# Channel mixers of a two-layer trunk: five plain hidden tiles in place of seven, and the down-projection's units placed by a list

## The chip, the cores and the metric

The kernel runs on one core of a Trainium2 chip. Its engines are TensorE (PE; its weight loads are listed apart as PEld), VectorE (DVE), ScalarE (ACT), GpSimd (POOL) and SyncE (SP), and in this kernel SP issues the weight loads. Every engine takes its own instructions in order; semaphores order the engines against each other. The metric is the device time of one execution in microseconds; a shorter time is better. Matmuls write into banks of PSUM, and ACT and DVE read from there.

## The reference, cut to what matters

The trunk has two layers. Each has a mixer over the sequence (a matrix memory in the first, banded attention in the second, both with attention to a memory) and then a channel mixer, on 512 tokens of width 1024 in float32. Only the channel mixers are touched by the change:

```python
D_FF = ((8 * D_MODEL // 3 + 127) // 128) * 128      # 2816, 22 tiles of 128
def conv_ffn(h, w_up, conv_w, conv_b, w_down):
    u, g = jnp.split(h @ w_up, 2, axis=-1)
    g = causal_dwconv(g, conv_w, conv_b)
    return (jax.nn.silu(g) * u) @ w_down
...
x = x + conv_ffn(rmsnorm(x, norm_ffn_g[l]), ffn_w_up[l], ffn_conv_w[l], ffn_conv_b[l], ffn_w_down[l])
```

So every hidden tile needs a gate product and an up product over all 1024 inputs, a causal convolution of width 3 along the sequence on the gate, a silu, and a multiplication. The 22 hidden tiles together then go through the down-projection.

## The kernel before

**Arithmetic.** A float32 product is made of three matmuls (`mm3`, L165 to L169): high by high, high by low, low by high. For that every weight tile and every activation is split in two: ACT casts the high half (L133), DVE subtracts it for the low half (L134). Weights arrive as raw float32 in a buffer of the pool `wr` (`load`), and `parts` splits them into a buffer of `wh` and one of `wl`; each of the three pools has three buffers. SP issues the loads in the order of the program, and a load waits until the split that last read its buffer is done. PSUM banks come from three pools, `mm` (three), `sc` (three) and `tr` (two), shown in the profile as `pmm`, `psc` and `ptr`.

**A channel mixer** (`ChannelMixer`, run once per layer, in the trace from about 285 to 605 us and from about 852 to 1170 us) takes the 22 hidden tiles in two ways.

*Plain tiles* (`plain`, the first seven): gate and up are each 8 × 3 matmuls of 128 × 512, 48 in a tile. The first four tiles use the unscaled input and multiply by the norm's row afterwards, on DVE (`L678`, `L684`); the later ones use the scaled forms in `ready`. The generator `forms` makes these: for each of the eight input tiles one multiply on DVE (`L693`) and a split, and then for four pairs the sums that Winograd's scheme wants (`L711`, halves of 256 columns) and their splits. `weave` mixes it into the plain tiles at a given rate. In this stage a scheduler orders the instructions.

*Winograd steps* (`step`, tiles 7 to 21): gate and up of a tile, seen as a 2 × 2 block product, take seven products instead of eight. A product is 4 × 3 matmuls of 128 × 256, 84 in a step. The weight sums and their splits for the next step are made meanwhile on DVE and ACT (`Forms`), and so is the convolution of the previous tile (`Tail`). In this stage the order of the code is the order of the instructions on PE, ACT and DVE (`manual_schedule`). The products go into three banks, `r1`, `r2` and `r3`. The middle of a step, with the lines of the profile:

```python
self.products(new.r3, w.s1, self.t(1), True)                       # L807
w.add_down(0)
then(tail, "split")
then(nxt, "split_up")
self.products(r1, w.s3, self.t(3))                                 # L811
A.copy(new.u3[:, :H], r1[:, :H])                                   # L812
V.tensor_tensor(out=new.pre[:, H:], in0=new.u3[:, :H], in1=new.r3[:, :H], op=ALU.add)   # L813
then(nxt, "split_sums")
w.down_products(1)
then(nxt, "sum_fourth")
w.add_down(1)
self.products(r1, w.a22, self.t(4))                                # L818
A.copy(new.pre[:, :H], r1[:, :H])                                  # L819
then(nxt, "split_down", "split_gate")
self.products(new.r3, w.s4, self.b(1, 1))
```

The product `a22` adds onto the same bank `r1` that the copy at L812 reads.

**The down-projection** of the first 16 hidden tiles is cut into 16 units. Unit q takes four hidden tiles (`GROUP`) and two output tiles: a load of 512 KB, a split, and two halves of 12 matmuls of 128 × 512 (`down_products`, in a `tr` bank). ACT copies each half out (`L735`), and POOL adds it to the output's spill with an accumulating transfer (`L736`). Units 0 and 1 stand behind plain tiles 5 and 6, units 2 to 15 in steps 7 to 20, one half after the product `s2` and one between `s3` and `a22`; step 21 has none. A unit's weights are loaded and split a step ahead. The last six hidden tiles go through their own final projection behind the mixer, whose matmuls the scheduler also puts into step 21.

`beside` issues, once per step, the transfers on POOL that build the bias rows of the later attention; only the first mixer has any.

Of the kernel before, what the change touches and what calls it, by code (L numbers as in the profile page):

```python
# [19 lines left out]
KT = D // P  # L20
# [18 lines left out]

PLAIN, UNSCALED, GROUP, LAST = 7, 4, 4, 6
H = S // 2


# [5 lines left out]
def trunk(  # L51
# [61 lines left out]
    for i, sel in enumerate(sels):  # L113
        G.memset(f(sel), 0.0)
        for s in (2 * i, 2 * i + 1):
            q = slice(32 * s, 32 * s + AH)
# [34 lines left out]
    def parts(raw, pinned=False):  # L151
        _, a, b = raw.shape
        hi = sb("wh", [P, D], F32R)[:, : a * b].rearrange("p (a b) -> p a b", a=a)
        lo = sb("wl", [P, D], F32R)[:, : a * b].rearrange("p (a b) -> p a b", a=a)
        split(hi, lo, raw, pinned=pinned)
        return hi, lo
# [25 lines left out]
    def run(gen):  # L182
        while True:
            try:
                next(gen)
            except StopIteration as end:
                return end.value

    def chain(*gens):
        for g in gens:  # L190
            yield from g
# [6 lines left out]
    def weave(job, filler, each, lead=0):  # L198

        due = lead  # L200
        for n in chain([0], job):
            due += each if n is None else each * n
            while due >= 1:
                due -= 1
                next(filler, None)

    def until(there, filler):
        while not there():
            next(filler)
# [35 lines left out]
    class Norm:  # L245


        def __init__(self):
            self.acc = self.row = None
# [154 lines left out]
    def reload_x():  # L404
        for j in range(KT):
            xT[j] = sb("u", [P, S])
            tc.keep_in_program_order(nc.sync.dma_start(xT[j], xspill[j]))
# [416 lines left out]
    class Forms:  # L824


        def __init__(self, mixer, j):
            self.mixer, n = mixer, KT // 2
            self.q = j - GROUP - 1
            self.up, self.gate = mixer.load_pair(j)  # L830
            self.raw_down = mixer.load_down(self.q) if self.q < 4 * n else None
            self.s13 = mixer.s[:, :D].rearrange("p (a b) -> p a b", a=KT)
            self.s24 = mixer.s[:, D : 2 * D].rearrange("p (a b) -> p a b", a=KT)

# [80 lines left out]
    def channel_mixer(l, act, norm, gain, beside):  # L915

        mixer = ChannelMixer(l, act, norm, gain, beside)
        forms = mixer.forms()
        run(mixer.plain(0))
        for j in range(1, UNSCALED):  # L920
            weave(mixer.plain(j), forms, KT / (16.0 * (UNSCALED - 1)))
        until(lambda: len(mixer.ready) == KT, forms) if len(mixer.ready) < KT else None
        mixer.buffers()
        for j in range(UNSCALED, PLAIN):
            q = j - GROUP - 1
            raw = mixer.load_down(q) if q >= 0 else None
            weave(mixer.plain(j), forms, 4 / (16.0 * 2))
            if raw is not None:
                w = parts(raw)
                for i in range(2):  # L930
                    mixer.add(*mixer.down_products(q, i, w))
        run(forms)
        mixer.later()
        reload_x()
        return mixer.hid[FT - LAST :]
# [289 lines left out]
    def more_rows():  # L1225
        if len(reps) < BH:
            bias_rows()

    hid = channel_mixer(0, act, norm, col["gffn"][:, 0:8], more_rows)
    norm2, kvact, act = Norm(), [], []  # L1230
    for j in range(KT):
# [161 lines left out]
    def final_norm(T):  # L1393
# [11 lines left out]
        nc.sync.dma_start(out[T * P : (T + 1) * P, S:], xt[T][1])  # L1405

    hid = channel_mixer(1, act, norm, col["gffn"][:, 8:16], lambda: None)
    n = LAST // 2
    for hf in range(2):
# [76 lines left out]
```

## Time and profile before

| | |
|---|---|
| median of 3 runs | 1211.17 us (1210.78 to 1211.25) |
| profiled execution | 1212.1 us, its span 1210.3 us |
| granted clock of TensorE, mean | 0.999 |
| PE busy | 1197.6 us, 99% of the span |
| PEld busy | 1054.6 us, 87% |
| DVE busy | 934.3 us, 77% |
| ACT busy | 693.0 us, 57% |
| POOL busy | 115.7 us, 10% |

The median is taken over runs without the profiler; the profile is of one further execution. The span is the time from the first to the last instruction of the trace. Engines' busy times overlap, so they don't add up to the span. A row of the timeline reads: start in us from the span's beginning, duration in us, engine, line, operation, tile written <- tiles read, shape; in brackets the idle time of the engine just before, and what released it. Matmuls are pipelined: a row's duration is longer than the distance to the next matmul's start, and that distance is the price of one. In a table of stretches (`A:B`) stand the length, then each engine's busy time with the number of its instructions, PE's granted clock, the share of the DMA engines and the GB/s.

### The profile page before, as it was taken

The page shows a single profiled execution, that of the slowest core. Times are in us where ns is not written, and L with a number is a line of the kernel's source. Part 1 is how long each engine was busy: PE and PEld are TensorE (multiplying, and loading weights), DVE is VectorE, ACT ScalarE, POOL GpSimd, SP SyncE. Part 2 cuts the span into 40 slices and gives each one's busy share as a digit, 9 for nine tenths or more (in the row PEclk, how much of TensorE's full clock was granted, in tenths as well). Part 3 has the DMA queues.
Part 4 walks back from the last instruction along what each step waited for, and adds up shares of the span by engine and source line. Part 5 has one row for each costly group of instructions (what it writes and reads, how often), then busy time and mean ns, then how long its engine had stood idle before and what let it go on. Part 6 is the DMA issues. An engine that isn't in the chain of part 4 may idle for free.

```text
span 1210.3 us, 18434 instructions
## 1 busy us (share of the span) xinstructions
PE 1197.6 (99%) x6919; PEld 1054.6 (87%) x6919; DVE 934.3 (77%) x1703; ACT 693.0 (57%) x1217; POOL 115.7 (10%) x191
## 2 busy tenths in 40 slices
PE   9999999999999999999999999999999999999997
PEld 8888888888889999999988888888888999999986
DVE  7878678878976777777788888997886677777755
ACT  4536567644545555555575767776464555555545
POOL 1300000000001111111011100001000101111100
PEclk9999999999999999999999999999999999999999
DMA  8634221444346667666563323236424666665551
GB/s 276 200 105 106 69 53 56 140 129 147 98 111 150 150 158 155 158 155 145 135 201 111 93 82 87 64 125 201 127 76 122 133 137 139 140 138 135 121 156 70
DMA packets 199019, 155.98 MB, mean 129 GB/s; under 512 B 7864, under 2 KB 179346, under 8 KB 198930
## 3 DMA queue, kind: packets, MB, share of 16 engines
q1 hardware_dynamic: 184338, 120.78, 34.0%
q0 software_dynamic: 14592, 34.03, 14.4%
q8 instruction: 54, 0.88, 0.3%
q14 instruction: 35, 0.29, 0.1%
HBM read 126.27 MB, written 32.44 MB: 131 GB/s over the span
## 4 chain that ended last, share of the span: by engine, by line
PE 92%; ACT 3%; DVE 3%; issue 0%; DMA 0%; SPq 0%; DVEq 0%; ACTq 0%
PE pmm L167 17%; PE pmm L169 17%; PE pmm L168 17%; PE ptr L167 6%; PE ptr L168 6%; PE ptr L169 6%; PE psc L167 6%; PE psc L169 6%; PE psc L168 6%; PE psc L505 2%; PE ptr L1313 1%; PE ptr L1334 1%; PE ptr L1335 1%; ACT wh L133 1%; DMA u<-in_mem_dram 0%
## 5 line engine op out<-in xcount | busy, mean ns | idle before, releaser
L167 PE MATMUL pmm<-u,wh 128*128 128x512 f32 (+1 forms) x952 | 336.0, 353 | 0.1
L169 PE MATMUL pmm<-u,wl 128*128 128x512 f32 (+1 forms) x952 | 332.5, 350 | 0.0
L168 PE MATMUL pmm<-u,wh 128*128 128x512 f32 (+1 forms) x952 | 332.2, 349 | 0.1
L134 DVE TENSOR_TENSOR wl<-wr,wh 128x1024 fp32r<-128x1024 f32 (+4 forms) x178 | 206.9, 1163 | 119.6 <-ACT wh L133 118.8
L133 ACT CAST wh<-wr 128x1024 fp32r<-128x1024 f32 (+4 forms) x178 | 178.4, 1004 | 131.6 <-PE pmm L168 50.3
L169 PEld LDWEIGHTS pmm<-u,wl 128*128 128x128 f32 x952 | 180.4, 189 | 22.3
L168 PEld LDWEIGHTS pmm<-u,wh 128*128 128x128 f32 x952 | 180.7, 190 | 19.3 <-DVE u L134 0.8
L167 PEld LDWEIGHTS pmm<-u,wh 128*128 128x128 f32 x952 | 180.5, 190 | 18.9 <-ACT u L133 0.5
L167 PE MATMUL ptr<-u,wh 128*128 128x512 f32 x272 | 106.7, 392 | 0.0
L168 PE MATMUL ptr<-u,wh 128*128 128x512 f32 x272 | 106.5, 392 | 0.0
L169 PE MATMUL ptr<-u,wl 128*128 128x512 f32 x272 | 105.8, 389 | 0.0
L736 POOL DMA_DIRECT2D xspill<-t x64 | 55.6, 868 | 472.6 <-ACT t L735 462.2
L167 PE MATMUL psc<-u,wh 128*128 128x512 f32 (+1 forms) x248 | 84.0, 339 | 0.0
L169 PE MATMUL psc<-u,wl 128*128 128x512 f32 (+1 forms) x248 | 83.8, 338 | 0.0
L168 PE MATMUL psc<-u,wh 128*128 128x512 f32 (+1 forms) x248 | 83.8, 338 | 0.0
L169 PE MATMUL pmm<-u,u 128*128 128x256 f32 x264 | 74.9, 284 | 0.2 <-DVE u L134 0.2
L167 PE MATMUL pmm<-u,u 128*128 128x256 f32 x264 | 75.0, 284 | 0.0
L168 PE MATMUL pmm<-u,u 128*128 128x256 f32 x264 | 74.8, 283 | 0.0
L735 ACT COPY t<-ptr 128x512 f32<-128x512 f32 x64 | 37.5, 586 | 63.2 <-PE ptr L169 63.2
L134 DVE TENSOR_TENSOR u<-t,u 128x512 fp32r<-128x512 f32 x78 | 53.4, 689 | 19.0 <-ACT u L133 18.7
L134 DVE TENSOR_TENSOR u<-pt,u 128x512 fp32r<-128x512 f32 x90 | 61.7, 689 | 5.1 <-ACT u L133 3.0
L133 ACT CAST u<-pt 128x512 fp32r<-128x512 f32 x90 | 55.4, 618 | 9.9 <-DVE pt L845 9.8
(285 smaller groups left out, 2431.2 us busy)
## 6 DMA issues: line engine op xcount, KB each, us to landing
wr<-in_ffn_w_up_dram SPq DMA_DIRECT2D x58, 512.0 KB, 4.6
wr<-in_ffn_w_down_dram SPq DMA_DIRECT2D x38, 512.0 KB, 3.7
xspill<-t POOLq DMA_DIRECT2D x64, 256.0 KB, 4.6
pt<-in_ffn_w_up_dram SPq DMA_DIRECT2D x30, 512.0 KB, 6.6
wr<-in_a_w_in_dram SPq DMA_DIRECT2D x20, 512.0 KB, 3.9
xspill<-u POOLq DMA_DIRECT2D x32, 256.0 KB, 3.0
u<-xspill SPq DMA_DIRECT2D x32, 256.0 KB, 5.1
wr<-in_w_kv_dram SPq DMA_DIRECT2D x12, 512.0 KB, 4.0
```

The source lines that it names most:

```text
L133: high = A.copy(hi, src) if on_act else V.tensor_copy(hi, src)
L134: low = V.tensor_tensor(out=lo, in0=src, in1=f(hi), op=ALU.subtract)
L167: nc.tensor.matmul(o, lh, rh, start=first, stop=False, skip_group_check=more)
L168: nc.tensor.matmul(o, lh, rl, start=False, stop=False, skip_group_check=more)
L169: nc.tensor.matmul(o, ll, rh, start=False, stop=last, skip_group_check=more)
L505: nc.tensor.matmul(o, a, b, start=first and i == 0, stop=i == 1)
L735: A.copy(t, o)
L736: G.dma_start(xspill[j], t, accum_op=ALU.add)
L1313: nc.tensor.transpose(tp[:, b * P : (b + 1) * P], es[T, h][:, b * P : (b + 1) * P], ident)
L1334: nc.tensor.matmul(o2[:, s * P :], w, hi_at(pts[h], s, s, TT - s), start=s == 0, stop=False)
L1335: nc.tensor.matmul(o2[:, s * P :], w, lo_at(pts[h], s, s, TT - s), start=False, stop=s == TT - 1)
```

## The change

Five plain tiles in place of seven, of which three instead of four are unscaled; tiles 5 and 6 become Winograd steps, so there are 17 steps instead of 15. A list `DOWN` says where each of the 16 units stands: units 0 and 1 both behind plain tile 4, unit 2 in step 6, unit 3 in step 8, units 4 to 15 in steps 9 to 20. Steps 5, 7 and 21 have none. The weights of units 0 and 1 are both loaded ahead of tile 4's. The eight scaled forms are woven into tiles 1 and 2 instead of 1 to 3, and the sums into tiles 3 and 4 instead of 4 and 5, at the same rate as before. `until` is called without its condition; it then draws from `forms` only while forms are missing, as before. Lines of the changed kernel are one to three higher than those of the kernel before.

```diff
-PLAIN, UNSCALED, GROUP, LAST = 7, 4, 4, 6
+PLAIN, UNSCALED, GROUP, LAST = 5, 3, 4, 6
+DOWN = (4, 4, 6, 8, *range(9, 21))
 H = S // 2
...
             self.mixer, n = mixer, KT // 2
-            self.q = j - GROUP - 1
             self.up, self.gate = mixer.load_pair(j)
-            self.raw_down = mixer.load_down(self.q) if self.q < 4 * n else None
+            self.raw_down = None
+            if j in DOWN:
+                self.q = DOWN.index(j)
+                self.raw_down = mixer.load_down(self.q)
...
         for j in range(1, UNSCALED):
             weave(mixer.plain(j), forms, KT / (16.0 * (UNSCALED - 1)))
-        until(lambda: len(mixer.ready) == KT, forms) if len(mixer.ready) < KT else None
+        until(lambda: len(mixer.ready) == KT, forms)
         mixer.buffers()
         for j in range(UNSCALED, PLAIN):
-            q = j - GROUP - 1
-            raw = mixer.load_down(q) if q >= 0 else None
-            weave(mixer.plain(j), forms, 4 / (16.0 * 2))
-            if raw is not None:
+            raws = {q: mixer.load_down(q) for q in range(len(DOWN)) if DOWN[q] == j}
+            weave(mixer.plain(j), forms, 4 / (16.0 * (PLAIN - UNSCALED)))
+            for q, raw in raws.items():
                 w = parts(raw)
                 for i in range(2):
                     mixer.add(*mixer.down_products(q, i, w))
```

## The prediction

> **What bounds the kernel now.** I read the page first, then the table of stretches and the list of waits for the two channel mixers, then the timeline around the first steps.
>
> ```profile
> span 1210.3 us, 18434 instructions
> PE 1197.6 (99%) x6919; PEld 1054.6 (87%) x6919; DVE 934.3 (77%) x1703; ACT 693.0 (57%) x1217; POOL 115.7 (10%) x191
> PEclk9999999999999999999999999999999999999999
> PE 92%; ACT 3%; DVE 3%; issue 0%; DMA 0%; SPq 0%; DVEq 0%; ACTq 0%
> ```
>
> TensorE (PE) is busy 99% of the span at a granted clock of nine tenths or more in every slice, and the chain that ended last is 92% PE. So an edit saves what it takes out of PE's own stream and costs what it makes PE wait. The two stages that it touches show this more sharply. In the table of stretches, one regular step with a down-projection unit and a stretch of the plain tiles read:
>
> ```profile
> core 0: us, PE busy (x) PEld busy (x) DVE busy (x) ACT busy (x) POOL busy (x), PEclk, DMA share, GB/s
> 294.40:319.80 25.40, 25.40 (x114) 21.01 (x113) 24.41 (x35) 14.94 (x21) 0.00 (x0) 1.00 0.33 99
> 371.67:387.22 15.55, 15.55 (x110) 14.56 (x108) 7.71 (x10) 7.55 (x13) 4.37 (x6) 1.00 0.68 156
> 387.22:402.77 15.55, 15.55 (x110) 14.57 (x109) 11.74 (x17) 8.80 (x17) 2.93 (x4) 1.00 0.67 156
> ```
>
> PE has no gap in any of them. DVE, 7.71 to 11.74 us of 15.55 in a step, has 24.41 of 25.40 us in the early plain tiles: there it is nearly as full as PE. The list of PE's waits has no entry between 285 and 605 us, nor between 852 and 1170 us. Nothing stalls before; the question is what stalls after.
>
> **1. Two plain tiles fewer, two Winograd steps more, in each mixer.** The timeline gives all prices of PE (first matmuls of plain tiles 3 and 4, of steps 7 and 8, and the edges of the two down halves of step 7):
>
> ```profile
> 317.26 0.39 PE L167 MATMUL pmm<-u,wh 128*128 128x512 f32 x1
> 328.14 0.39 PE L167 MATMUL pmm<-u,wh 128*128 128x512 f32 x1
> 371.67 0.28 PE L167 MATMUL pmm<-u,wh 128*128 128x256 f32 x1
> 375.98 0.40 PE L167 MATMUL ptr<-u,wh 128*128 128x512 f32 x1
> 378.73 0.28 PE L167 MATMUL psc<-u,wh 128*128 128x256 f32 x1
> 381.48 0.28 PE L169 MATMUL pmm<-u,wl 128*128 128x256 f32 x1
> 381.60 0.40 PE L167 MATMUL ptr<-u,wh 128*128 128x512 f32 x1
> 384.35 0.28 PE L167 MATMUL pmm<-u,u 128*128 128x256 f32 x1
> 387.22 0.28 PE L167 MATMUL pmm<-u,wh 128*128 128x256 f32 x1
> ```
>
> A plain tile takes 328.14 − 317.26 = 10.88 us, 48 matmuls of 512 columns. A step with its unit takes 387.22 − 371.67 = 15.55, its two down halves 378.73 − 375.98 and 384.35 − 381.60, 2.75 each; so its own 84 matmuls of 256 columns take 15.55 − 5.50 = 10.05. Each converted tile saves 10.88 − 10.05 = 0.83 us, four of them (two per mixer, two mixers) **3.3 us**. Number and price of the down units stay as they are, as do the final projections.
>
> The saving rests on 0.1196 us for a 256-column matmul (10.05 / 84) beside 0.2267 for 512 columns (10.88 / 48). The Trainium skill, "TensorE: Matmul & The Clock Gate", section "Wait — 56ns, not 53.3ns?", gives start-to-start as N over 2.4 GHz plus about 2.5 ns on a warm array. By that page, as an estimate, the pair would be 109 and 216 ns, a tile would save 1.2 us and the four 4.7. Both sizes are dearer here, the small one by more, so the measurement decides.
>
> **2. Steps without a down unit: a new wait on PE.** Only three units move. Before, q = 0 and 1 stand behind plain tiles 5 and 6 and q = 2 in step 7; after, 0 and 1 stand behind tile 4 and q = 2 in step 6. From step 8 on every step has the unit it had. Steps 5 and 7 have none, and this takes away what stands between product s3 (L811) and product a22 (L818). Both write the bank r1, and ACT's copy at L812 must read it between them. In step 7 of before:
>
> ```profile
> 381.80 0.37 ACT L812 COPY t<-pmm 128x256 f32<-128x256 f32 x1 [1.34 <-PE pmm L169]
> 382.20 0.42 DVE L813 TENSOR_TENSOR t<-t,psc 128x256 f32<-128x256 f32 x1 [0.49 <-ACT t L812]
> ```
>
> The last matmul of s3 starts at 381.48, the copy starts at 381.80, and what it releases can start at 382.20. The down half from 381.60 to 384.35 covers all of this. With no half there, a22 would want to start at 381.60 and be let go at 382.20: 0.60 us idle. Step 21, the one step of before that has no unit, shows the wait itself:
>
> ```profile
> 596.58 0.28 PE L169 MATMUL pmm<-u,wl 128*128 128x256 f32 x1
> 596.70 0.40 PE L167 MATMUL pmm<-u,wh 128*128 128x512 f32 x1
> 596.78 0.83 ACT L133 CAST wh<-wr 128x768 fp32r<-128x768 f32 x1 [0.93 <-PE pmm L168]
> 597.52 0.37 ACT L812 COPY t<-pmm 128x256 f32<-128x256 f32 x1
> 597.93 0.19 PEld L167 LDWEIGHTS pmm<-u,u 128*128 128x128 f32 x1 [0.35 <-ACT t L812]
> 597.93 0.39 PE L167 MATMUL pmm<-u,u 128*128 128x256 f32 x1
> 598.16 0.28 PE L168 MATMUL pmm<-u,u 128*128 128x256 f32 x1
> ```
>
> There a22's weight load is released by L812 at 597.93; PE meanwhile ran matmuls of the final projection, which steps 5 and 7 do not have at hand. It also shows the restart: 0.23 from the first to the second matmul, 0.11 above the usual 0.12. So a bare step costs 0.60 + 0.11 = 0.71 us, and four cost **2.8 us**. Bounds: nothing, if a22 need not wait (rival 1), and 597.93 − 596.70 = 1.23 each, 4.9 in all, if a cast stands ahead of the copy on ACT as it does in step 21. I take 0.71, because the casts of a regular step stand elsewhere: ACT was idle for 1.34 us when L812 began. The other waits on r1 keep a product of about 1.4 us between them.
>
> DVE in a bare step: step 5 is a first step, without the previous tile's taps, so it has the 7.71 us of the third row of the table beside 10.05 of PE. Step 7 has up to 11.74, more than PE's 10.05. DVE enters with slack, because step 6 leaves it 15.55. But its add at L813, which s4 waits for, then comes about 0.1 late: **0.2 us** for both mixers, with 0 and 11.74 − 10.05 − 0.71 = 1.0 each as ends.
>
> **3. Two raw down loads ahead of tile 4.** This is the tightest place. `load` has three raw buffers. Units 0 and 1 are now loaded before tile 4's weights and hold two of them until their splits, which stand behind tile 4's on DVE. So gate 4 and up 4 go one after the other through the third: load, cast, low half, next load. Before, two buffers took turns. The rows that price it:
>
> ```profile
> 294.35 0.69 DVE L678 TENSOR_TENSOR t<-pmm,rb 128x512 f32<-128x512 f32 x1
> 303.19 1.22 DVE L134 TENSOR_TENSOR wl<-wr,wh 128x1024 fp32r<-128x1024 f32 x1
> 304.32 0.68 DVE L134 TENSOR_TENSOR u<-t,u 128x512 fp32r<-128x512 f32 x1
> 304.92 0.74 DVE L645 SCALAR_TENSOR_TENSOR t<-t,cols,t 128x511 f32<-128x511 f32 x1
> 305.58 0.68 DVE L134 TENSOR_TENSOR u<-u,u 128x512 fp32r<-128x512 f32 x1
> 317.24 1.06 ACT L133 CAST wh<-wr 128x1024 fp32r<-128x1024 f32 x1
> 318.55 1.21 DVE L134 TENSOR_TENSOR wl<-wr,wh 128x1024 fp32r<-128x1024 f32 x1
> 319.79 0.37 SPq L146 DMA_DIRECT2D wr<-in_ffn_w_up_dram  x1
> 323.51 0.42 DVE L711 TENSOR_TENSOR t<-u 128x256 f32<-128x256 f32 x1
> 323.85 0.42 DVE L711 TENSOR_TENSOR t<-u,u 128x256 f32<-128x256 f32 x1
> DMA to landing us min/median/max: 3.4/3.8/4.9
> ```
>
> The first ten are timeline rows; the last is what the `wr` tiles between 308 and 353 us answer. Back to back, DVE takes 1.13 for a low half of 1024, 0.60 for a 512 subtract, 0.66 for a 512 multiply-add, 0.34 for a 256 subtract. The input's scaled forms now finish within tiles 1 and 2 instead of 1 to 3, so more stands ahead of up 3's low half. From 294.35 on I count 14 multiply-adds, 3 low halves of 1024, 19 subtracts or multiplies of 512 and 4 of 256 in the changed order: 9.24 + 3.39 + 11.40 + 1.36 = 25.39, so that low half starts at 319.74 (318.55 before) and ends at 320.95. The next load leaves 0.03 later (318.55 + 1.21 to 319.79). One round is 3.8 for landing, 1.06 cast, 1.21 low half and some 0.12 of hand-overs: 6.19. Gate 4 is ready at 327.14, before tile 4 wants it at 328.14, and up 4 at 333.33. PE wants up 4's low half with the third matmul of its 25th to 48th, at 328.14 + 5.44 + 0.45 = 334.03, and loads those weights one matmul earlier, at 333.80. That leaves 0.47 us, the same in both mixers. The count of DVE carries an error of a few tenths, so I take **0.1 us** per mixer, 0.2 in all; ends 0 and, with the slowest landing of the row twice, 2 × (4.9 − 3.8) − 0.47 = 1.7 per mixer.
>
> The Trainium skill, "DMA: Bandwidth & Descriptors", section "Anatomy of one DMA", states a fixed cost of about 2 us beside the bytes over 436 GB/s; for 512 KB that is, as an estimate, 3.2 us. By it up 4 would have over a microsecond to spare and the sum would be 0.2 lower. The row shows 3.8.
>
> **4. What costs nothing.** Each moved unit brings its SP load, one cast (1.06), one low half (1.21), two L735 copies and two accumulating POOL transfers along. Behind tile 4 they lie where 11 us of down products cover them, in step 6 beside 15.55 us of PE. SP issues in order, and behind up 4 stand only up 5 and what follows, wanted after those 11 us. Without that cover a unit would cost its load and split, 6 us once. The bias transfers on POOL in the first mixer start two steps earlier; POOL has 4.37 us in a step. The `until` without its condition issues nothing.
>
> **Sum.** −3.3 + 2.8 + 0.2 + 0.2 = −0.1 us on the profiled execution of 1212.1 (span 1210.3). The median of the runs, 1211.17, stands 0.9 below it, so 1212.0 for a profiled execution and **1211.1** for the median. About 0.2%, 2.4 us, is what a measurement of this kernel can tell from no change.
>
> **The rivals.**
>
> *Rival 1, faster: the bare steps cost nothing.* a22 accumulates on r1, but if L812 were done in time, or PE had other work, −3.3 + 0.2 would remain: 1208.0. Against it: the 597.93 row, and 382.20 against 381.60. For it: only that no step of before stands bare without filler, so the idle time itself has never been seen.
>
> *Rival 2, slower: the single raw buffer makes up 4 late.* Place: start of up 4, 334 us and again in the second mixer. Each microsecond beyond the 0.47 of margin passes to PE whole, and twice. With 4.9 per landing it gives 2 × 1.7 = 3.4 in place of 0.2: 1214.3. It decides once two landings together with DVE's lateness exceed 0.47; a slowdown over 0.2% wants a wait of about 1.4 in each mixer. For it: DVE full to 24.41 of 25.40 ahead of the chain. Against: the loads run alone there, and the median is 3.8.
>
> *Rival 3: DVE bounds step 7.* 1.0 in place of 0.1 in each mixer: 1212.9, still no change that can be told.
>
> *Rival 4: a cast on ACT ahead of L812 in the bare steps,* as in step 21: 1.23 + 0.11 in place of 0.71, 2.5 more: 1213.6, at the edge of slower.
>
> **How the numbers follow.** My sum, 0.54; rival 1, 0.10; rival 2, 0.18; rival 3, 0.08; rival 4, 0.06, half of it slower; waits that I did not find, 0.04, slower. So faster 0.10, within 0.2% 0.65, slower 0.25. The likeliest alone spans 1210 to 1212.5. For 8 in 10 the range takes in rivals 2 to 4 and stops above rival 1: 1208.6 to 1214.8.
>
> **What would show it.** Steps 5 and 7: a gap of 0.6 to 0.8 us before a22, put down to ACT L812, four times, and none in step 6. First matmuls of steps 5 and 6 about 10.7 apart. Tile 4: up 4's low half ending near 333.3, PE's wait for it 0 to 0.3. PE with 144 more matmuls. From step 9 on the same spacing as before. The prediction is wrong if a22 follows s3 at once, or if PE waits over a microsecond for a weight split in tile 4 or for DVE in step 7.

## The result and the profile after

The changed kernel takes 1213.15 us (median of 12 runs) against 1211.36 for the kernel before (12 runs): 1.0016 times the time, 95% interval 1.0009 to 1.0024. A second set, 11 runs against 33, gave 1212.29 against 1210.98: 1.0012 (1.0003 to 1.0021). By the medians the change costs 1.3 to 1.8 us, 0.11 to 0.15%. I had forecast −0.1, and a time within 0.2%: the size lies inside that, the sign is wrong, and neither interval holds a ratio of 1.

The page of the changed kernel, the lines that answer to those shown of before:

```profile
span 1211.5 us, 18772 instructions
PE 1195.4 (99%) x7063; PEld 1059.0 (87%) x7063; DVE 951.6 (79%) x1739; ACT 704.2 (58%) x1245; POOL 115.4 (10%) x191
PE 94%; ACT 3%; DVE 2%; DMA 0%; issue 0%; SPq 0%; ACTq 0%; DVEq 0%
```

PE has 144 more matmuls and is busy 2.2 us less; the span is longer all the same. The list of PE's waits has one new row, and it is the one that the prediction named, L812 of before being L813 now (line, what it waited for, us in total, times, longest):

```profile
PE pmm L168 <- ACT t L813: 2.5, 4, 0.7
```

The table of stretches of the changed kernel shows the down products behind tile 4, then steps 5, 6 and 7 (length, then busy time of PE, PEld, DVE, ACT, POOL):

```profile
338.77:349.65 10.88, 10.88 (x49) 9.01 (x48) 8.19 (x12) 5.99 (x9) 2.60 (x3) 1.00 0.64 153
349.65:360.49 10.84, 10.32 (x85) 10.12 (x84) 6.30 (x9) 5.46 (x10) 2.54 (x4) 1.00 0.70 147
360.49:376.05 15.56, 15.56 (x110) 14.58 (x109) 12.06 (x18) 8.81 (x17) 2.91 (x4) 1.00 0.57 139
376.05:387.26 11.21, 10.48 (x87) 10.18 (x85) 10.00 (x16) 6.93 (x13) 1.17 (x3) 1.00 0.64 158
```

PE idles in steps 5 and 7 only. 84 matmuls at 0.12 are 10.08 us, so step 5 is 0.76 too long and step 7 1.13. The timeline around the two gaps:

```profile
356.72 0.28 PE L170 MATMUL pmm<-u,wl 128*128 128x256 f32 x1
357.10 0.37 ACT L813 COPY t<-pmm 128x256 f32<-128x256 f32 x1 [0.95 <-PE pmm L170]
357.52 0.39 PE L168 MATMUL pmm<-u,u 128*128 128x256 f32 x1 [0.52 <-ACT t L813]
...
382.77 1.04 ACT L134 CAST wh<-wr 128x1024 fp32r<-128x1024 f32 x1
383.13 0.28 PE L170 MATMUL pmm<-u,wl 128*128 128x256 f32 x1
383.72 0.36 ACT L813 COPY t<-pmm 128x256 f32<-128x256 f32 x1
384.14 0.38 PE L168 MATMUL pmm<-u,u 128*128 128x256 f32 x1 [0.73 <-ACT t L813]
```

In step 5 the last matmul of s3 starts at 356.72 and a22 at 357.52: 0.80 instead of 0.12, with ACT idle before the copy. In step 7 ACT is inside a cast when s3 ends, so the copy starts 0.59 after s3's last matmul instead of 0.38, and a22 1.01 after it. Step 7 has one more wait, of the last product s4 for DVE's add (L813 of before):

```profile
385.25 0.41 DVE L814 TENSOR_TENSOR t<-t,psc 128x256 f32<-128x256 f32 x1
385.54 0.28 PE L170 MATMUL pmm<-u,u 128*128 128x256 f32 x1
385.72 0.39 PE L168 MATMUL psc<-u,u 128*128 128x256 f32 x1
385.94 0.28 PE L169 MATMUL psc<-u,u 128*128 128x256 f32 x1
```

s4 starts 0.18 after the last matmul of a22 instead of 0.12, and its second matmul 0.22 after the first: some 0.15 in all. The 1.13 of step 7 are thus about 0.99 ahead of a22 (1.01 − 0.12 and 0.10 for the slow second matmul) and 0.15 ahead of s4.

How much of the whole is that? DVE's copy at L290 (now L291) marks the same point ahead of tile 1 of each mixer and in the second layer's first norm. Of the kernel before, then of the changed one:

```profile
293.63 0.69 DVE L290 COPY rb<-psc 128x512 f32<-128x512 f32 x1 [0.98 <-PE psc L242]
643.35 0.69 DVE L290 COPY rb<-psc 128x512 f32<-128x512 f32 x1 [0.69 <-PE psc L242]
859.88 0.69 DVE L290 COPY rb<-psc 128x512 f32<-128x512 f32 x1 [0.98 <-PE psc L242]
1203.13 0.28 PE L169 MATMUL pmm<-wh,u 128*128 128x256 f32 x1
```

```profile
293.37 0.69 DVE L291 COPY rb<-psc 128x512 f32<-128x512 f32 x1 [0.98 <-PE psc L243]
643.35 0.69 DVE L291 COPY rb<-psc 128x512 f32<-128x512 f32 x1 [0.69 <-PE psc L243]
859.86 0.69 DVE L291 COPY rb<-psc 128x512 f32<-128x512 f32 x1 [0.98 <-PE psc L243]
1203.36 0.28 PE L170 MATMUL pmm<-wh,u 128*128 128x256 f32 x1
```

The stretch with the first mixer grew from 349.72 to 349.98, the one with the second (to the last matmul of the program) from 343.25 to 343.50: +0.26 and +0.25, some 0.5 us in all. The layer between them did not move (216.53, 216.51). But from the start of the last matmul to the end of the span it is 1210.3 − 1203.1 = 7.2 us before and 1211.5 − 1203.4 = 8.1 after. **Nothing in the diff touches that end, and it costs more than both mixers.** The transfers there, of before and of after (1206 to 1210 us of the span; the issues' columns are count, KB and median us to landing):

```profile
q1 hardware_dynamic: 288, 0.52, 34.0%
issues: line engine op xcount, KB each, median us to landing
out_dram<-u SPq DMA_DIRECT2D x2, 256.0 KB, 2.3
```

```profile
q1 hardware_dynamic: 288, 0.52, 34.9%
q14 instruction: 1, 0.01, 0.5%
issues: line engine op xcount, KB each, median us to landing
out_dram<-u SPq DMA_DIRECT2D x2, 256.0 KB, 3.2
```

The last output write takes 3.2 us to land instead of 2.3, and among the packets is one that is no data: a fetch of instructions. Packet by packet, counted from the start of the last matmul, all data have been moved by 5.51 us before. After, the fetch stands at 5.02 to 5.33, and the last seven packets of data run one behind another until 6.31. SP waits for this write before the program ends.

### The profile page after: what moved, and what is told of

Read it like the earlier page. It is cut to its first block, busy times and chain, and to the rows that moved or that the text cites. A ratio compares the mean times of both kernels' runs of the same rounds, so it can differ in the third digit from the quotient of the medians.

```text
span 1211.5 us, 18772 instructions
## 1 busy us (share of the span) xinstructions
PE 1195.4 (99%) x7063; PEld 1059.0 (87%) x7063; DVE 951.6 (79%) x1739; ACT 704.2 (58%) x1245; POOL 115.4 (10%) x191
## 4 chain that ended last, share of the span: by engine, by line
PE 94%; ACT 3%; DVE 2%; DMA 0%; issue 0%; SPq 0%; ACTq 0%; DVEq 0%
PE pmm L168 18%; PE pmm L170 18%; PE pmm L169 18%; PE ptr L168 6%; PE ptr L169 6%; PE ptr L170 6%; PE psc L168 5%; PE psc L170 5%; PE psc L169 5%; PE psc L506 2%; PE ptr L1315 1%; ACT wh L134 1%; PE ptr L1336 1%; PE ptr L1337 1%; PE ptr L575 0%; PE ptr L589 0%
## 5 line engine op out<-in xcount | busy, mean ns | idle before, releaser
L135 DVE TENSOR_TENSOR wl<-wr,wh 128x1024 fp32r<-128x1024 f32 (+4 forms) x174 | 202.0, 1162 | 97.1 <-ACT wh L134 96.3
L134 ACT CAST wh<-wr 128x1024 fp32r<-128x1024 f32 (+4 forms) x174 | 174.1, 1002 | 106.0 <-PE pmm L169 47.2
L170 PEld LDWEIGHTS pmm<-u,wl 128*128 128x128 f32 x968 | 183.6, 190 | 21.1
L169 PEld LDWEIGHTS pmm<-u,wh 128*128 128x128 f32 x968 | 183.9, 190 | 18.0 <-DVE u L135 0.8
L168 PEld LDWEIGHTS pmm<-u,wh 128*128 128x128 f32 x968 | 183.7, 190 | 17.7 <-ACT u L134 0.5
L168 PE MATMUL pmm<-u,u 128*128 128x256 f32 x296 | 84.5, 285 | 2.5 <-ACT t L813 2.5
L170 PE MATMUL pmm<-u,u 128*128 128x256 f32 x296 | 83.9, 283 | 0.2 <-DVE u L135 0.2
L169 PE MATMUL pmm<-u,u 128*128 128x256 f32 x296 | 83.8, 283 | 0.0
L135 DVE TENSOR_TENSOR u<-pt,u 128x512 fp32r<-128x512 f32 x102 | 70.2, 688 | 9.7 <-ACT u L134 7.0
L168 PE MATMUL psc<-u,wh 128*128 128x256 f32 (+1 forms) x232 | 76.1, 328 | 0.0
L170 PE MATMUL psc<-u,wl 128*128 128x256 f32 (+1 forms) x232 | 75.9, 327 | 0.0
L169 PE MATMUL psc<-u,wh 128*128 128x256 f32 (+1 forms) x232 | 75.9, 327 | 0.0
L134 ACT CAST u<-pt 128x512 fp32r<-128x512 f32 x102 | 63.0, 617 | 11.3 <-DVE pt L848 11.3
```

What stands on the lines that cost most here:

```text
L134: high = A.copy(hi, src) if on_act else V.tensor_copy(hi, src)
L135: low = V.tensor_tensor(out=lo, in0=src, in1=f(hi), op=ALU.subtract)
L168: nc.tensor.matmul(o, lh, rh, start=first, stop=False, skip_group_check=more)
L169: nc.tensor.matmul(o, lh, rl, start=False, stop=False, skip_group_check=more)
L170: nc.tensor.matmul(o, ll, rh, start=False, stop=last, skip_group_check=more)
```

## The experiments

Theory 1: the stalls in steps 5 and 7 nearly eat the saving, and the rest is outside the mixers. Theory 2: the added steps cost something everywhere. All were timed beside the kernel before on one chip in each set.

**The kernel before against itself.**

> The kernel before, unchanged, against itself: how far two sets of runs of one program lie apart, and a second trace of it. Both theories: ratio 1.0000, medians within 0.5 us. If its own medians lie 1 us apart, the +1.8 us of the changed kernel is partly no property of the change. The second trace shows which parts of the span differ from one execution to the next; I expect them ahead of the first 10 us and behind the last matmul, up to 1 us, and the channel mixers equal to 0.05 us.

1.0001 (0.9992 to 1.0010), 1211.05 against 1210.98. Its trace has 349.69 and 343.23 us in the two stretches, 0.03 from the first trace. But the first mixer's mark is at 292.07 instead of 293.63: 1.6 us between two executions of one program, all ahead of the first mixer. Of these 1.6 us, 1.5 are there already at the first L290 copy, at 35.09 and 33.62; I had expected up to 1 us, and part of it at the end, which is 7.20 in both. So spans of single executions can't be compared to a microsecond; stretches can.

**The changed kernel again.** No edit.

> The changed kernel again, with a second trace. The first trace showed idle time of PE of 0.79 and 1.16 us in steps 5 and 7 of each mixer beside a saving of 1.6, so +0.3 per mixer, while the runs showed +1.8 us in all. Theory 1, the stalls are the whole cost and the rest is scatter outside the mixers: about +0.6 us to the kernel before, 1212.0. Theory 2, the changed program pays another 1.2 us somewhere else: +1.8 again, and the trace has a place for it.

+1.3 us, with 349.99 and 343.53 in the stretches, the same gaps (0.68 and 0.88 beyond a matmul's distance) and again 8.11 from the last matmul to the end, the last write landing after 3.18. The long end belongs to the program, not to one execution. Theory 2 is right in that there is another place, and wrong on what it is: it is no cost of a step.

**Work of PE between s3 and a22.**

```diff
-            self.products(new.r3, w.s1, self.t(1), True)
+            bare, n = w.raw_down is None and j < FT - 1, KT // 2
+            self.products(new.r3, w.s1, self.t(1), True, range(n // 2) if bare else None)
...
             self.products(r1, w.s3, self.t(3))
+            if bare:
+                self.products(new.r3, w.s1, self.t(1), True, range(n // 2, n))
             A.copy(new.u3[:, :H], r1[:, :H])
```

> The changed kernel with one edit: in steps 5 and 7 the second half of product s1 (6 matmuls, 0.72 us) stands between s3 and a22, so that ACT's copy of r1 has work of PE beside it. Same instructions, same result. If the copy is what PE waits for in these steps, the gap before a22 goes in step 5 (0.8 to under 0.1) and mostly in step 7 (1.16 to about 0.4, since a cast still stands ahead of the copy there and DVE is late for s4). Theory 1: 2.8 us below the changed kernel at the least, about 1208.7, 2.5 below the kernel before. Theory 2: the same step down, but from 1213.2, so about 1210.2. If the step is DVE's to set and not the copy's, nothing changes.

1210.04, ratio 0.9993 (0.9984 to 1.0002): 2.25 us below the changed kernel, though not 2.8. Its steps 5 and 7:

```profile
348.57:358.71 10.14, 10.14 (x85) 10.13 (x84) 6.21 (x9) 5.47 (x10) 2.54 (x4) 1.00 0.70 150
374.27:385.46 11.19, 10.71 (x86) 10.22 (x85) 9.98 (x16) 6.90 (x13) 1.67 (x3) 1.00 0.60 156
```

Step 5 lost its stall (10.84 to 10.14): there the copy was the cause. Step 7 as a whole lost nothing (11.21 to 11.19), though I had expected most of its gap to go. From start to start, its wait ahead of a22 fell from 1.01 to 0.69, but a new one of 0.35 stands ahead of s3: the half of s1 that moved had covered ACT's copy of `r1` between s2 and s3 (L803). Step 5 accounts for 2 × 0.70 = 1.4 of the 2.25; most of the rest is the end, which is 7.20 here.

**One plain tile fewer and a unit in every step.**

```diff
-PLAIN, UNSCALED, GROUP, LAST = 5, 3, 4, 6
-DOWN = (4, 4, 6, 8, *range(9, 21))
+PLAIN, UNSCALED, GROUP, LAST = 6, 4, 4, 6
+DOWN = (5, 6, 7, 8, *range(9, 21))
```

> One plain tile fewer instead of two, and a unit in every step: PLAIN 6, UNSCALED 4, units 0 behind tile 5, 1 to 3 in steps 6 to 8. No step is bare, so no gap; it saves 0.8 us in each mixer if the price of a step (10.08) against a plain tile (10.88) is right. Theory 1: 1.6 below the kernel before, 1209.8. Theory 2, a cost that comes with each added step (1.2 us for four of them, 0.6 for two): 1.0 below, 1210.4.

1209.44 against 1210.98, −1.5: 0.9990 (0.9981 to 0.9999). The stretches are 348.95 and 342.47, −0.75 and −0.77 for one tile each. Here a step with its unit, 15.55, stands in place of a plain tile, 10.88, and a unit behind one, 5.44 (half of the 10.88 from 338.77 on): 0.77 by the prices. With every step covered a converted tile is worth what its matmuls say, and an added step costs nothing else. Theory 2's cost in each step falls.

**Step 7: order or volume?**

```diff
-            then(tail, "split")
-            then(nxt, "split_up")
+            if not bare:
+                then(tail, "split")
+                then(nxt, "split_up")
...
+            if bare:
+                then(nxt, "split_up")
+                then(tail, "split")
             then(nxt, "split_sums")
```

> split_s1 with one more edit: in steps 5 and 7 the previous tile's split and the next tile's up split stand behind the add to the convolution's input instead of ahead of s3. In split_s1 step 5 fell from 10.84 to 10.14 us, but step 7 stayed at 11.19 (11.21 in the changed kernel): its waits only moved. Theory A, order: ACT's copies in step 7 wait behind casts that wait for DVE; then step 7 falls to 10.3 to 10.5 and the kernel to 1208.7, 1.4 below split_s1. Theory B, volume: DVE has more work in step 7 than the step lasts without a unit (11.1 against 10.08), in whatever order; then step 7 stays near 11.1 or step 8 takes the wait over, and the time stays at 1210.0.

1208.64 against 1211.47: 0.9976 (0.9966 to 0.9986), 2.8 us faster than the kernel before. Steps 5 and 7:

```profile
349.14:359.27 10.13, 10.13 (x86) 10.12 (x85) 5.47 (x8) 5.35 (x10) 2.54 (x4) 1.00 0.70 151
374.83:385.22 10.39, 10.32 (x86) 10.12 (x85) 8.79 (x15) 6.16 (x12) 1.13 (x2) 1.00 0.71 173
```

Step 7 is 10.39, and the stretches are 348.47 and 342.00: 1.2 us less in each mixer than before the change. It was the order, not the volume. The edit moves casts on ACT and subtractions on DVE together; the timeline of `split_s1` shows what a22 waited for there:

```profile
380.99 1.05 ACT L134 CAST wh<-wr 128x1024 fp32r<-128x1024 f32 x1
381.67 0.28 PE L170 MATMUL psc<-u,wl 128*128 128x256 f32 x1
381.94 0.36 ACT L816 COPY t<-pmm 128x256 f32<-128x256 f32 x1
382.36 0.39 PE L168 MATMUL pmm<-u,u 128*128 128x256 f32 x1 [0.41 <-ACT t L816]
```

The cast of the next up weights was on ACT until 382.04, the copy that a22 needs came behind it, and a22 started 0.69 after the last matmul of s1 instead of 0.12. What is left in step 7 of `late_casts`, 0.3, is the wait ahead of s3 that moving half of s1 had opened; ACT's silu precedes the copy of `r1` there:

```profile
379.15 0.63 ACT L917 ACTIVATE t<-t 128x512 f32<-128x512 f32 x1 [2.31 <-DVE t L646]
379.69 0.35 ACT L803 COPY t<-pmm 128x256 f32<-128x256 f32 x1
379.75 0.28 PE L170 MATMUL psc<-u,wl 128*128 128x256 f32 x1
380.10 0.39 PE L168 MATMUL pmm<-u,wh 128*128 128x256 f32 x1
```

**One unit behind tile 4 instead of two.** `DOWN = (4, 5, 6, 8, ...)` in the kernel just shown.

> late_casts with unit 1 in step 5 instead of behind tile 4: only step 7 is bare, and the stretch of down products behind tile 4 is 5.44 us instead of 10.88. If the change's second unit behind tile 4 covers nothing that one unit doesn't cover, step 5 loses its 0.06 of stall and nothing else moves: 0 to 0.1 below late_casts. If step 5's weight sums and splits need the 10.88 us, PE waits at its start, up to 5 us in each mixer.

1209.12, 0.9979 (0.9970 to 0.9988); stretches 348.53 and 342.00, those of the kernel with two units to 0.06. The runs show no gain over that kernel (0.9976, with overlapping intervals), where 0 to 0.1 us had been expected. One unit's 5.44 us covers step 5's sums and splits; the second one covers nothing that needs it.

**The end: four DVE instructions more in the changed kernel, thirty in the one before** (there the condition is `j >= 7`).

```diff
+            if j in (12, 14):
+                V.memset(padt, 0.0)
             new = Tail(self, j)
```

> The changed kernel with 2 tiny DVE memsets in each mixer (of a 128x1 tile that nothing reads, in steps 12 and 14, where DVE has time): 4 DVE instructions more, as many as split_s1 has. Both traces of the changed kernel show a fetch of 8 KB of instructions among the packets of the last output write, and an end 0.91 us longer than in all the other traces (8.11 against 7.20 from the last matmul to the end of the span). Theory: the place of this fetch hangs on the count of DVE's instructions; with 4 more it comes some 10 us earlier, the end is 7.20 again and the time 0.9 below the changed kernel, +0.4 to the kernel before. Rival: it hangs on another engine's count or on the order in the mixers; then the end stays 8.11 and the time +1.3.

> The kernel before with one such memset in each of steps 7 to 21 of both mixers, 30 in all: DVE then has 2116 instructions in the program, as many as in the changed kernel, and nothing else differs. If the fetch at the end hangs on DVE's count, this kernel gets the long end, 8.11, and the time 0.9 above the kernel before. If it hangs on another engine, the time stays within 0.3 of it. The memsets themselves cost nothing where PE is the bound.

Both came out on the side of DVE's count. With the instructions that only wait included, the traces list 2084 of DVE for the kernel before, 2114 for the changed one and as many for the kernel before with 30 memsets (the expectation has 2116 for both), and 2118 for the changed one with 4. The changed kernel with 4 memsets: 1211.76 against 1211.47, 1.0002 (0.9993 to 1.0010); its end is 7.20 us and its stretches still 350.00 and 343.52, so the mixers' loss is all there and the end's is gone. The kernel before with 30: 1212.65, 1.0009 (1.0000 to 1.0018), with untouched stretches (349.69, 343.18) and the long end, 8.11. The interval of its runs just touches 1; the end in the trace is what decides. Its transfers in the same four microseconds of its trace:

```profile
q1 hardware_dynamic: 288, 0.52, 35.3%
q14 instruction: 1, 0.01, 0.5%
issues: line engine op xcount, KB each, median us to landing
out_dram<-u SPq DMA_DIRECT2D x2, 256.0 KB, 3.2
```

So thirty instructions that do no work make the kernel before nearly as slow as the changed one, with not a matmul moved.

The account, against the kernel before (stretches against the mean of its two traces, 349.70 and 343.24; end against 7.20; the changed kernel by its first trace; all in us):

| kernel | mixer 1 | mixer 2 | end | sum | runs |
|---|---|---|---|---|---|
| changed | +0.28 | +0.26 | +0.91 | +1.45 | +1.79, +1.31 |
| split_s1 | −0.38 | −0.45 | 0 | −0.83 | −0.94 |
| plain6 | −0.75 | −0.77 | 0 | −1.52 | −1.54 |
| late_casts | −1.23 | −1.24 | 0 | −2.47 | −2.83 |
| one_bare | −1.17 | −1.24 | 0 | −2.41 | −2.35 |
| pad_after | +0.30 | +0.28 | 0 | +0.58 | +0.29 |
| pad_before | −0.01 | −0.06 | +0.91 | +0.84 | +1.18 |

The sums from single traces agree with the runs to 0.4 us.

## Why the prediction was right or wrong

In the mixers the mechanism was the one named, and two terms of the sum were mis-sized: the bare step 7 above all, and the saving. The larger part of the slowdown came from the end of the program, for which the sum has no term. That the time lies within the stated range says little: the range is 6 us wide, and the measured difference is 1.3 to 1.8.

*Saving of a converted tile.* 0.83 forecast. I had subtracted two down halves of 2.75 from a step, and a half behind a plain tile takes 2.72; 84 matmuls at 0.12 are 10.08, not 10.05, so a bare step saves 0.80 by the matmuls, and four tiles give 3.2 instead of 3.3. The 0.75 to 0.77 of `plain6` is the price where the added step carries a unit, as said there.

*Bare step 5.* 0.71 forecast, 0.76 measured, by the mechanism named, and removed by giving PE work there.

*Bare step 7.* 0.71 for a22 and 0.1 for s4 forecast, 0.99 and 0.15 measured, 1.13 together: 0.3 us too little in each mixer, nearly all of it ahead of a22. The failed step is "the casts of a regular step stand elsewhere: ACT was idle for 1.34 us when L812 began". That was read in step 7 of before, a first step, which has no previous tile and so no silu, no taps and no split of it on ACT and DVE. In the changed kernel the first step is step 5, and there the reading held; step 7 is a regular one. ACT there is inside a cast of 1024 columns when s3 ends. Rival 4's mechanism was at work in half of the bare steps. Of its price only a part came: 0.99 against 1.34. Rival 3, DVE as the bound of step 7, falls: its 0.15 is close to the 0.1 that the sum had, and `late_casts` has step 7 at 10.39 with the same instructions in another order.

*The single raw buffer.* Up 4's low half was forecast to end at 333.33, in a trace whose marks lie 0.26 later than those of the changed kernel's:

```profile
331.83 1.23 DVE L135 TENSOR_TENSOR wl<-wr,wh 128x1024 fp32r<-128x1024 f32 x1 [0.49 <-ACT wh L134]
333.79 0.39 PE L170 MATMUL psc<-u,wl 128*128 128x512 f32 x1
```

It ends at 333.06, and 0.26 more is 333.32. PE takes it at 333.79 without waiting; the 0.1 per mixer that I allowed was not needed, and rival 2 falls. Counting DVE's instructions in the changed order by their distances from the trace of before came out 0.05 off at up 3's low half (forecast to start at 319.74, in the trace 319.53 and 0.26 more). That the end of the chain agrees to 0.01 is in part luck: gate 4's low half ended 0.11 late, at 326.99 and 0.26 more instead of 327.14, and up 4's round was as much shorter. The Trainium skill, "DMA: Bandwidth & Descriptors", section "Anatomy of one DMA", gives the fixed cost and the rate that I used for transfers that GpSimd issues. These loads are issued by SP, so the 3.2 us was no rival to the 3.8 of the row.

*What costs nothing.* Loads, POOL transfers and the earlier bias rows cost nothing, as said: the list of PE's waits has no row of theirs in the mixers. So the mixers' sum, −0.1 forecast, becomes −3.2 + 3.8 = +0.6: the saving is 0.1 smaller, the bare steps cost 2 × (0.76 + 1.13) = 3.8 instead of 3.0, and up 4 costs nothing instead of 0.2. The two stretches show +0.5.

*The end.* No step of the prediction held it: the sum takes everything outside the mixers as unchanged, without a reason, and the rivals were all drawn within them. The changed number of instructions itself moved a fetch, +0.91 us, two thirds of the traced slowdown. That alone takes the measured difference from one that the runs can't resolve (pad_after, 1.0002) to one that they can.

## What to carry to other kernels

When work moves between steps, look at what it stood in front of: a matmul group that hid the copy out of a PSUM bank, which the next group needs, was paying for itself. In step 5 half a product, 0.72 us of independent work, closed such a gap; but ask what that half covered where it stood before, for in step 7 it opened 0.3 us there. The copy that releases PE goes ahead of casts that nobody waits for yet. Read an engine's idle time in a step of the kind that the change will make, not in the first one of a loop; and where less than 0.2% matters, compare the span from mark to mark, and the end by itself.

## What the runs showed of the hardware

Fetches of instructions stand among the data in the lists of transfers, and one can hold up data. Queue 8 fetches 16 KB at a time, 54 times in the kernel before and 55 times in the changed one, which has 144 matmuls and 144 weight loads more; I take it for PE's. Queue 14 fetches 8 KB at a time. One such fetch put the landing of the last write from 2.27 to 3.18 us, in all three traces with 2114 instructions of DVE. In the three with 2118 (`split_s1`, `late_casts`, `pad_after`) it comes 3.0 us before the last matmul, about ten before the end; there it puts an earlier write from 2.31 to between 3.04 and 3.10, and nothing waits for that one. With 2109 (`one_bare`) it comes 1.6 us behind the end of the span.

The traces also tell whose fetch it is. The kernel before with 30 memsets differs from the kernel before in DVE's instructions alone. Of its fetches of 8 KB in the last 360 us five lie within 0.5 us of where they were, counted from the last matmul; four come 6 to 20 us earlier, and the one at the end is new. These five lie 121 to 140 of DVE's instructions apart, so they are DVE's. The Trainium skill, "Runtime: NRT & Kernel Launch", section "Instruction fetch mechanics", says that an engine's sequencer fetches the next block over its own DMA queue while it works on the present one, in blocks of 16 KB, and that this is mostly hidden. On queue 8 the block agrees; on queue 14 it was 8 KB here; and hidden it is, until it falls on a transfer that something waits for. What sets the moment of the fetch, beyond its change with DVE's count, stays open.

The time ahead of the first mixer differs by up to 1.6 us between executions of the same work (its mark lies between 292.07 and 293.63 in the ten traces), while the stretches of the mixers, where the program is the same there, repeat to 0.07. Most of the scatter of the runs can be of that kind; that is not shown.
